# Reading the mLSTM normalisers ahead of all stages and loading each head's state matrix one background step before the sample chunk, in a one-core Trainium2 encoder layer

## The chip, the core and the metric

The kernel is one program on one core of one Trainium2 chip. The metric is the device time of one execution in microseconds (us), lower is better; the time of a kernel is the median of its runs. The engines of the core are named as the profile names them: PE (TensorE, matrix products; PEld is its weight load), DVE (VectorE), ACT (ScalarE), POOL (GpSimd) and SP (SyncE), whose queue issues every DMA of this kernel.

## The reference

One layer of a streaming encoder is computed for two streams: a prompt of 1024 tokens without history, and a sample of 64 tokens that continues a running stream. What matters here is the mLSTM branch: four heads of width 256, each with a matrix memory `C` (256 x 256), a normaliser `n` (256) and a running maximum `m`. A chunk of tokens reads the old memory and writes the new one:

```python
s = einsum(q, k) * w_intra
num = einsum(s, v) + w_inter[..., None] * einsum(q, C0)
den = sum(s, axis=-1) + w_inter * einsum(q, n0)
h = num / maximum(abs(den), exp(-m))[..., None]
C1 = decay * C0 + einsum(w_end, k, v)
n1 = decay * n0 + einsum(w_end, k)
```

For the prompt `C0`, `n0` start at zero. For the sample they are the inputs `state_C` and `state_n`. Both streams' final `C`, `n` and `m` are outputs.

## The kernel before

**Chunks.** The 1088 tokens of both streams (1024 and 64) stand side by side in the token dimension and are cut into three chunks of 384, 384 and 320. The input projection runs as units: one unit is one 128-column piece of `w_in`, and for each of the three chunks 24 matrix products (8 pieces of the contraction, three split products each, lines 326, 329 and 330) go into one PSUM tile `g` (three buffers). An operand is split into a high part (`...h`, by ACT) and a low part (`...l`, by DVE); `split`, lines 334 and 337, does both. So ACT writes `wh`, `Ch`, `smh` and DVE then writes `wl`, `Cl`, `sml`.

**Background steps.** After each chunk of a unit, `slot()` runs one step of the mLSTM generator of the current head, some steps of the depthwise convolution (each one DVE operation `acc` on 128x1118 elements) and one of a third generator. An mLSTM head takes nine chunks of 128 tokens (`c` = 0 to 7 the prompt, `c` = 8 the sample, 64 tokens) with two steps each. The first step of a chunk makes the products of q and k (`pS`), transposes k (`pk`) and prepares `sm`, `smh`, `sml`, `kwh`, `kwl`. The second transposes the last chunk's output (`out_gate`), then makes 15 products of width 258: three with `smh`/`sml` (`pN`), six with `Ch`/`Cl` (`pI`, the old memory), six with `kwh`/`kwl` (`pC`, the new memory), from which DVE writes the new `C`. So between two steps PE does the 24 products of a chunk.

**The state of the sample.** A tile `C` holds `C` in columns 0 to 255, `n` in column 256, and zeros behind. It has two buffers. After the second step of `c` = 7, lines 503 and 504 write the prompt's `C` and `n` out, the latter as 256 elements of 4 bytes. The first step of `c` = 8 takes the buffer that is free, loads `state_C` (256 KB, line 456) and `state_n` (256 elements of 4 bytes, line 457) into it and splits it (`csplit`).

**Order.** The program is written once and a scheduler orders each engine's instructions at build time; on the chip each engine goes through its own list strictly in order and waits at an instruction until what it needs is there. SP issues all DMAs in one list, and each takes the next of eight completion lanes in turn (`DMAHW0` to `DMAHW7` in the order's rows): an issue waits until the lane's earlier DMA has landed.

**Start.** `start_x` transposes x, loads the small vectors into rows of `vp` (`w_dw` first, then six rows), then the convolution cache `cp`. Behind these on SP stand a piece of `w_in` (`wr`, line 1109), the gate weights (into `fa`, line 219), the gate bias `bgb` and `state_m` (`smc`). `gates()` copies the gate weights into `wg` and multiplies (lines 238, 239).

Of the kernel before, what the change touches and what calls it, by code (L numbers as in the profile page):

```python
# [9 lines left out]
F32 = mybir.dt.float32  # L10
# [11 lines left out]
P = 128  # L22
KT = D // P
NH = 4
HD = 256
# [24 lines left out]
def hybrid_layer(ctx, tc, x_prompt, x_sample, cache_conv, state_C, state_n, state_m, w_in, b_gate,  # L50
# [3 lines left out]
    nc = tc.nc  # L54
    V, S, G, TE = nc.vector, nc.scalar, nc.gpsimd, nc.tensor
    w_in = w_in[0]

    def pool(name, bufs=1, stack=ctx, **kw):
        kw.setdefault("reuse_waits", "tile")
        if kw.get("space") is DRAM:  # L60
            kw.pop("reuse_waits")
        return stack.enter_context(tc.tile_pool(name=name, bufs=bufs, **kw))

    const = pool("const")
# [19 lines left out]
    def mtile():  # L84
        return pools["psm"].tile([P, 512], F32, tag="m", name="m")
# [37 lines left out]
            CREDIT["conv"] -= 1.0  # L123
        step("misc")

# [1 line left out]
    ident = const.tile([P, P], F32, name="ident")  # L127
    make_identity(nc, ident)
    vecs = const.tile([P, KT, NV], F32, name="vecs")
# [9 lines left out]
    dec = const.tile([P, NH, NT], F32, name="dec")  # L139
    bgb = const.tile([P, 8], F32, name="bgb")  # L140
    smc = const.tile([P, 1], F32, name="smc")

    proj = ExitStack()

# [1 line left out]
    XH, XL = [], []  # L146
    XO = {"h": XH, "l": XL}
    cv = pool("cv", stack=proj)
# [4 lines left out]
    def load_x(i):  # L153
        xt = xp.tile([P, D], F32, tag="x", name="x")
        nc.sync.dma_start(xt[:tile_len(i)], xrows(i))
        return xt

    def trans_x(i, xt):
        ci, off, n = i // 3, (i % 3) * P, tile_len(i)
        if i % 3 == 0:  # L160
            XH.append(ph.tile([P, KT, CN], F32R, tag="p", name="xh"))
            XL.append(pl.tile([P, KT, CN], F32R, tag="p", name="xl"))
        for kh in range(2):
            ps = mtile().rearrange("p (k t) -> p k t", k=4)
            for k in range(4):
                kk = kh * 4 + k
                TE.transpose(ps[:, k, :n], xt[:n, kk * P:(kk + 1) * P], ident[:n, :n])
            hi = XH[ci][:, kh * 4:kh * 4 + 4, off:off + n]
            S.activation(hi, ps[:, :, :n], AF.Copy)
            V.tensor_tensor(XL[ci][:, kh * 4:kh * 4 + 4, off:off + n], ps[:, :, :n], hi.bitcast(F32), ALU.subtract)  # L170
# [3 lines left out]
    def start_x():  # L174
        for i in range(3):
            trans_x(i, xt0[i])
            if i == 1:
                wsplit(0, True)
        for i in range(3, NT):
            trans_x(i, load_x(i))  # L180
        vp = xp.tile([NV, D], F32, tag="x", name="vp")
        nc.sync.dma_start(vp[0:CW, :], w_dw[0])
        for r, src in ((R_BDW, b_dw), (R_AG, ln_a_g), (R_AB, ln_a_b), (R_HN, hn_g), (R_G1, ln1_g), (R_B1, ln1_b)):
            nc.sync.dma_start(vp[r:r + 1, :], src[0:1, :])
        cp = xp.tile([CB, D], F32, tag="x", name="cp")
        nc.sync.dma_start(cp, cache_conv[0, 0])
        ps = mtile()
        for k in range(KT):
            TE.transpose(ps[:, k * NV:(k + 1) * NV], vp[:, k * P:(k + 1) * P], ident[:NV, :NV])
        V.tensor_copy(vecs, ps[:, :KT * NV].rearrange("p (k v) -> p k v", k=KT))  # L190
        ps = mtile()
        for k in range(KT):
            TE.transpose(ps[:, k * CB:(k + 1) * CB], cp[:, k * P:(k + 1) * P], ident[:CB, :CB])
        V.tensor_copy(cacheT, ps[:, :KT * CB].rearrange("p (k v) -> p k v", k=KT))

    N(start_x)

# [1 line left out]
    def gates():  # L199
        fa = fp.tile([P, 3072], F32, tag="f", name="fa")  # L200
        fb = fp.tile([P, 3072], F32, tag="f", name="fb")
# [102 lines left out]
            n = tile_len(b)  # L304
            V.tensor_copy(cols[:n, b:b + nb], ps[:n, 0:nb].rearrange("p c (h z) -> p c h z", z=32)[:, :, :, 0:4])

# [1 line left out]
    early, later = [], []  # L308

    def product(hi, lo, ci):  # L310
# [34 lines left out]
    def add_unit(w, c0, post):  # L345
        J(wcols(w, c0), lambda hi, lo: unit(hi, lo, post))

# [1 line left out]
    G32 = []  # L349
    HT = {}  # L350
    CVT = {}
# [67 lines left out]
    def mlstm(h):  # L419
        ml = pools["ml"]  # L420
        kf, qf, vh, vl, dt = HT["k"], HT["q"], HT["vh"], HT["vl"], HT["dt"]
        W = HD + 2
# [9 lines left out]

        def csplit(C):
            Ch = ml.tile([P, 2, W], F32R, tag="Ch", name="Ch")
            Cl = ml.tile([P, 2, W], F32R, tag="Cl", name="Cl")
            split(Ch, Cl, C)
            return Ch, Cl
# [7 lines left out]
                g = G32[ci][:, 2 * h + j, off:off + n]  # L445
                V.scalar_tensor_tensor(g, pT[:, j * P:j * P + n], vecs[:, 2 * h + j, R_HN:R_HN + 1], g, ALU.mult, ALU.mult)

        C = Ch = Cl = back = None
        nxt = prep(0)
        for c in range(NT):  # L450
            n, o = tile_len(c), c * P
            qs, ks = nxt
            if c == 8:
                C = ml.tile([P, 2, W], F32, tag="C", name="C", bufs=2)
                G.memset(C[:, :, HD + 1:], 0.0)
                nc.sync.dma_start(C[:, :, :HD], state_C[0, 0, h].rearrange("(j p) v -> p j v", p=P))
                nc.sync.dma_start(C[:, :, HD:HD + 1], state_n[0, 0, h].rearrange("(j p o) -> p j o", p=P, o=1))
                Ch, Cl = csplit(C)
            pS = mtile()
            for j in range(2):  # L460
                a = TE.matmul(pS[:, :2 * P], ks[:, j, 0, :], qs[:, j].rearrange("p e t -> p (e t)"), start=j == 0, stop=False)
# [38 lines left out]
            C = Cn  # L500
            if c >= 7:
                Cd, nd = (C_prompt, n_prompt) if c == 7 else (C_sample, n_sample)
                nc.sync.dma_start(Cd[0, 0, h].rearrange("(j p) v -> p j v", p=P), C[:, :, :HD])
                nc.sync.dma_start(nd[0, 0, h].rearrange("(j p o) -> p j o", p=P, o=1), C[:, :, HD:HD + 1])
            else:
                Ch, Cl = csplit(C)
            if c < 8:
# [13 lines left out]
            back = (c, n, isb)  # L521
# [97 lines left out]

    N(close_proj)  # L620

# [1 line left out]
    def set_operand(srcs, pad=False):  # L623
        H, L = [], []
        for ci, (_, n) in enumerate(CHUNKS):
# [18 lines left out]
        V.scalar_tensor_tensor(st[:n, 16:17], st[:n, 12:13], -1.0, st[:n, 15:16], ALU.mult, ALU.mult)  # L644
        return st[:n, 15:16], st[:n, 16:17]

# [1 line left out]
    A32, MB = [], []  # L648
    bra = ExitStack()

# [113 lines left out]
    for j in range(KT):  # L764
        add_unit(w_b_out[0], j * P, post_b(j))

# [1 line left out]
    wos = ExitStack()  # L768
    lns = ExitStack()
    WOH, WOL = [], []  # L770
# [23 lines left out]
    for j in range(KT):  # L794
        add_unit(w_a_out[0], j * P, post_ya(j))

# [1 line left out]
    X1H, X1L, Y2 = [], [], []  # L798
    last_ln = []

# [44 lines left out]

    N(out_proj)

# [1 line left out]
    stage[0] = 1  # L849
    NB = 4  # L850
    NBLK = 4 * KT // NB
# [156 lines left out]
        for jp in range(KT // 2):  # L1008
            wino_pair(blk, jp)

# [1 line left out]
    HID = {}  # L1012
    YT = []

# [82 lines left out]
        add_unit(w_ff1[0], u * P, post_h(u))  # L1097
    N(last_ff2)

# [1 line left out]
    pieces = [j for j in jobs if j[0] is not None]  # L1101
    raws, his = {}, {}
    now = [0]
# [7 lines left out]
    def wsplit(i, pinned=False):  # L1111
        if i < len(pieces) and i not in his and pieces[i][3] == now[0]:
            kind = pieces[i][2]
            w = KT * P if kind != "v" else 14 * P
            hi = pools["whl"].tile([P, w], F32R, tag="wh", name="wh")
            lo = pools["whl"].tile([P, w], F32R, tag="wl", name="wl")
            if kind != "v":
                split(hi, lo, raws[i], pinned=pinned)
                hi, lo = (t.rearrange("p (k n) -> p k n", n=P) for t in (hi, lo))
            else:  # L1120
                wino_weights(raws[i], hi, lo)
            his[i] = (hi, lo)
# [49 lines left out]
```

## Time and profile before

| | before |
|---|---|
| median of three runs | 2013.26 us (2011.92 to 2013.38) |
| the profiled execution's own span | 2012.8 us |
| PE busy | 1943.4 us, 97% |
| DVE busy | 1426.8 us, 71% |
| ACT busy | 648.7 us, 32% |
| POOL busy | 126.3 us, 6% |
| data moved by DMA | 131.06 MB, mean 65 GB/s |

The profile comes from one execution, 0.46 us shorter than the median, so durations from it can be set against the median as they are. A row of a time line has the start in us from the span's start, the duration, the engine, the line, the operation, out<-in with the tile names, and in square brackets the engine's idle time before it and what ended that. Matrix products are pipelined, so a product of 384 columns is shown with some 0.33 us while the next begins earlier. The granted clock of PE is 1.00 at 2.4 GHz and 0.50 at 1.2 GHz.

### The profile page before, as it was taken

The numbers are of one execution on the slowest core, as the hardware profiler recorded it, in microseconds if no ns is written. First come the engines' busy times: TensorE is split into PE (matmuls) and PEld (weight loads), VectorE is DVE, ScalarE is ACT, GpSimd is POOL, SyncE is SP. The second block draws the span as 40 slices with busy tenths as digits, with TensorE's granted clock in tenths as the row PEclk, the third lists the DMA queues.
The fourth block names the chain that finished last, engine by engine and source line by source line (L and its number), as shares of the span: only waits on it lengthen the run. The fifth ranks groups of instructions, "written<-read, shape, count | busy, mean of one in ns | idle before, by whom it ended". The sixth has DMA issues, their size and how long they took to land.

```text
span 2012.8 us, 30485 instructions
## 1 busy us (share of the span) xinstructions
PE 1943.4 (97%) x12395; PEld 1917.8 (95%) x12395; DVE 1426.8 (71%) x2717; ACT 648.7 (32%) x1209; POOL 126.3 (6%) x220
## 2 busy tenths in 40 slices
PE   8999899998999899989999998999999999999996
PEld 7999899998999899989999998999999999999995
DVE  4957776786678677868885557877686858677647
ACT  4323222333233323323342204524233332414232
POOL 1112210001000100000000000000000000000005
PEclk9999999999999999989999999999999999999998
DMA  4122321122112221225325310111111111111212
GB/s 148 44 78 67 85 70 43 54 67 47 56 41 63 62 63 37 64 66 172 116 82 154 116 40 21 32 53 43 53 42 54 43 43 53 43 53 43 74 42 79
DMA packets 174974, 131.06 MB, mean 65 GB/s; under 512 B 11518, under 2 KB 169694, under 8 KB 174833
## 3 DMA queue, kind: packets, MB, share of 16 engines
q1 hardware_dynamic: 174833, 129.11, 21.8%
q8 instruction: 97, 1.59, 0.3%
q14 instruction: 44, 0.36, 0.1%
HBM read 104.39 MB, written 24.63 MB: 64 GB/s over the span
## 4 chain that ended last, share of the span: by engine, by line
PE 80%; DVE 11%; DMA 4%; issue 2%; ACT 2%; POOL 1%; SPq 0%; POOLq 0%; ACTq 0%; DVEq 0%
PE g L326 25%; PE g L329 25%; PE g L330 25%; DMA C<-in_state_n_dram 2%; DVE s L668 2%; DVE acc L563 1%; PE m L326 1%; PE m L330 1%; PE m L329 1%; DVE o L1091 1%; DVE wl L337 1%; DVE ln L640 0%; DVE a L689 0%; DVE y L689 0%; DVE C L499 0%
## 5 line engine op out<-in xcount | busy, mean ns | idle before, releaser
L326 PE MATMUL g<-xh,wh 128*128 128x384 f32 (+1 forms) x1920 | 636.0, 331 | 0.0
L329 PE MATMUL g<-xl,wh 128*128 128x384 f32 (+1 forms) x1920 | 630.1, 328 | 0.0
L330 PE MATMUL g<-xh,wl 128*128 128x384 f32 (+1 forms) x1920 | 629.6, 328 | 0.0
L326 PEld LDWEIGHTS g<-xh,wh 128*128 128x128 f32 x1920 | 363.1, 189 | 0.4 <-ACT xh L334 0.2
L329 PEld LDWEIGHTS g<-xl,wh 128*128 128x128 f32 x1920 | 363.0, 189 | 0.3
L330 PEld LDWEIGHTS g<-xh,wl 128*128 128x128 f32 x1920 | 362.6, 189 | 0.1
L563 DVE SCALAR_TENSOR_TENSOR acc<-glu,vecs,acc 128x1118 f32<-128x1118 f32 x240 | 332.8, 1387 | 3.9
L334 ACT ACTIVATE wh<-wr 128x1024 fp32r<-128x1024 f32 (+1 forms) x168 | 166.1, 989 | 429.1 <-PE g L329 356.0
L337 DVE TENSOR_TENSOR wl<-wr,wh 128x1024 fp32r<-128x1024 f32 (+1 forms) x168 | 191.4, 1139 | 106.8 <-ACT wh L334 104.2
L326 PE MATMUL g<-x1h,wh 128*128 128x384 f32 (+1 forms) x768 | 253.1, 330 | 0.0
L329 PE MATMUL g<-x1l,wh 128*128 128x384 f32 (+1 forms) x768 | 252.8, 329 | 0.0
L330 PE MATMUL g<-x1h,wl 128*128 128x384 f32 (+1 forms) x768 | 252.6, 329 | 0.0
L329 PE MATMUL g<-hvl,wh 128*128 128x272 f32 x784 | 223.5, 288 | 0.0
L330 PE MATMUL g<-hvh,wl 128*128 128x272 f32 x784 | 221.5, 288 | 0.0
L326 PE MATMUL g<-hvh,wh 128*128 128x272 f32 x784 | 221.1, 289 | 0.1
L967 DVE TENSOR_TENSOR y<-g,y 128x272 f32<-128x272 f32 (+1 forms) x540 | 157.3, 341 | 26.8 <-PE g L330 25.1
L326 PEld LDWEIGHTS g<-hvh,wh 128*128 128x128 f32 x784 | 145.9, 189 | 1.7 <-DVE y L967 1.4
L329 PEld LDWEIGHTS g<-hvl,wh 128*128 128x128 f32 x784 | 147.4, 188 | 0.1
L330 PEld LDWEIGHTS g<-hvh,wl 128*128 128x128 f32 x784 | 146.4, 188 | 0.0
L330 PEld LDWEIGHTS g<-x1h,wl 128*128 128x128 f32 x768 | 144.8, 188 | 0.0
L329 PEld LDWEIGHTS g<-x1l,wh 128*128 128x128 f32 x768 | 144.7, 188 | 0.1
L326 PEld LDWEIGHTS g<-x1h,wh 128*128 128x128 f32 x768 | 144.5, 188 | 0.1
(267 smaller groups left out, 2440.9 us busy)
## 6 DMA issues: line engine op xcount, KB each, us to landing
wr<-in_w_in_dram SPq DMA_DIRECT2D x64, 512.0 KB
wr<-in_w_ff_dram SPq DMA_DIRECT2D x64, 512.0 KB
x<-in_x_prompt_dram SPq DMA_DIRECT2D x8, 512.0 KB
dwT<-acc SPq DMA_DIRECT2D x8, 512.0 KB
wr<-in_w_b_out_dram SPq DMA_DIRECT2D x8, 512.0 KB
wr<-in_w_a_out_dram SPq DMA_DIRECT2D x8, 512.0 KB
wr<-in_w_out_dram SPq DMA_DIRECT2D x8, 512.0 KB
out_dram<-o SPq DMA_DIRECT2D x16, 256.0 KB
```

What stands on the lines that cost most here:

```text
L326: first = TE.matmul(out, lh, rh, start=start, stop=False, skip_group_check=more)
L329: TE.matmul(out, lh, rl, start=False, stop=False, skip_group_check=more)
L330: TE.matmul(out, ll, rh, start=False, stop=stop, skip_group_check=more)
L334: a = S.activation(hi, src, AF.Copy)
L337: V.tensor_tensor(lo, src, hi.bitcast(F32), ALU.subtract)
L563: V.scalar_tensor_tensor(acc, glu[:, j:j + AC], vecs[:, c, j:j + 1], acc, ALU.mult, ALU.add))
L668: V.tensor_reduce(out[:, :n], t[:, :, :n].rearrange("p k t -> p t k"), AX.X, ALU.add)
L967: V.tensor_tensor(y, ps[:, pslc], y, ALU.add)
L1091: V.tensor_tensor(o[:n, hs], o[:n, hs], pools["g2"][:n, hs], ALU.mult)
```

## The change

`state_n` of all four heads goes into one small tile `snc`, by four loads in `start_x` between the rows of `vp` and `cp`. At the end of the second step of `c` = 7 the sample's tile is taken (`C0`), its matrix loaded, its last column zeroed and column 256 copied from `snc` on POOL. The sample chunk begins with an empty step (`yield`), and only then takes `C0` and splits it. The diff also removes comment lines, which stand as blank lines; these are left out below.

```diff
+    snc = const.tile([P, NH, 2], F32, name="snc")
...
             nc.sync.dma_start(vp[r:r + 1, :], src[0:1, :])
+        for h in range(NH):
+            nc.sync.dma_start(snc[:, h, :, None], state_n[0, 0, h].rearrange("(j p o) -> p j o", p=P, o=1))
         cp = xp.tile([CB, D], F32, tag="x", name="cp")
...
-        C = Ch = Cl = back = None
+        C = Ch = Cl = back = C0 = None
...
             if c == 8:
-                C = ml.tile([P, 2, W], F32, tag="C", name="C", bufs=2)
-                G.memset(C[:, :, HD + 1:], 0.0)
-                nc.sync.dma_start(C[:, :, :HD], state_C[0, 0, h].rearrange("(j p) v -> p j v", p=P))
-                nc.sync.dma_start(C[:, :, HD:HD + 1], state_n[0, 0, h].rearrange("(j p o) -> p j o", p=P, o=1))
+                yield
+                C = C0
                 Ch, Cl = csplit(C)
...
                 nc.sync.dma_start(nd[0, 0, h].rearrange("(j p o) -> p j o", p=P, o=1), C[:, :, HD:HD + 1])
+                if c == 7:
+                    C0 = ml.tile([P, 2, W], F32, tag="C", name="C", bufs=2)
+                    nc.sync.dma_start(C0[:, :, :HD], state_C[0, 0, h].rearrange("(j p) v -> p j v", p=P))
+                    G.memset(C0[:, :, HD + 1:], 0.0)
+                    G.tensor_copy(C0[:, :, HD:HD + 1], snc[:, h, :, None])
```

**PE, ahead of head 0's sample products.** Before, the last chunk in front of them ends so; each chunk of 24 products is shown by its last three rows, `m<-ident,isb` is `out_gate` of `c` = 7, `m<-vh,smh` the first of the 15 products:

```order
L326 MATMUL g<-xh,wh 128x320
L329 MATMUL g<-xl,wh 128x320
L330 MATMUL g<-xh,wl 128x320
L443 MATMUL m<-ident,isb 128x128 x2
L326 MATMUL m<-vh,smh 128x258
L329 MATMUL m<-vl,smh 128x258
L330 MATMUL m<-vh,sml 128x258
```

The same place after the change (lines are three or more higher):

```order
L329 MATMUL g<-xh,wh 128x320
L332 MATMUL g<-xl,wh 128x320
L333 MATMUL g<-xh,wl 128x320
L462 MATMUL m<-qs,ks 128x256
L465 MATMUL m<-qs,ks 128x128
L462 MATMUL m<-qs,ks 128x256
L465 MATMUL m<-qs,ks 128x128
L468 MATMUL m<-ident,k 128x128 x2
L329 MATMUL g<-xh,wh 128x384
L332 MATMUL g<-xl,wh 128x384
```

The products of q and k, which stood before the 320 chunk, now stand behind it, and a whole chunk of 384 stands between them and the sample's 15 products, in all four heads.

**ACT, around `Ch` of head 0's sample.** `s` is the eviction of a projection chunk, `wh` the split of the next weight piece, `sm` the first operation on the products of q and k. Before:

```order
L575 ACTIVATE s<-g 128x384
L471 ACTIVATE sm<-m 128x128
L339 ACTIVATE kwh<-m,cols 128x256
L334 ACTIVATE Ch<-C 128x516
L334 ACTIVATE smh<-sm 128x128
L334 ACTIVATE wh<-wr 128x1024
L575 ACTIVATE s<-g 128x320
```

After:

```order
L581 ACTIVATE s<-g 128x384
L337 ACTIVATE Ch<-C 128x516
L337 ACTIVATE wh<-wr 128x1024
L581 ACTIVATE s<-g 128x320
L472 ACTIVATE sm<-m 128x128
L342 ACTIVATE kwh<-m,cols 128x256
L337 ACTIVATE smh<-sm 128x128
```

`Ch`, which needs the loaded state, stood behind `sm` and `kwh`; it now stands ahead of both, with `wh` and an eviction between.

**DVE, the same place.** Before:

```order
L563 SCALAR_TENSOR_TENSOR acc<-glu,vecs,acc 128x1118
L472 TENSOR_TENSOR sm<-m,sm 128x128
L473 TENSOR_TENSOR sm<-sm,dt 128x128
L340 SCALAR_TENSOR_TENSOR kwl<-m,cols,kwh 128x256
L337 TENSOR_TENSOR Cl<-C,Ch 128x516
L337 TENSOR_TENSOR sml<-sm,smh 128x128
```

After:

```order
L340 TENSOR_TENSOR Cl<-C,Ch 128x516
L340 TENSOR_TENSOR wl<-wr,wh 128x1024
L473 TENSOR_TENSOR sm<-m,sm 128x128
L343 SCALAR_TENSOR_TENSOR kwl<-m,cols,kwh 128x256
L474 TENSOR_TENSOR sm<-sm,dt 128x128
L569 SCALAR_TENSOR_TENSOR acc<-glu,vecs,acc 128x1118
L340 TENSOR_TENSOR sml<-sm,smh 128x128
```

Here too `sm`, `kwl` and `sml` stood around `Cl`; they now stand behind it, `wl` and, for `sml`, `acc`.

**SP at the start, with what each issue waits for.** `DMAHW3_49` is the lane that the load of `w_dw` took. Before:

```order
L186 DMA cp<-in_cache_conv_dram 30x1024 [waits DMAHW2_49,PE_49]
L1109 DMA wr<-in_w_in_dram 128x8x128 [waits DMAHW3_49,DVE_49]
L219 DMA fa<-in_w_in_dram 128x8x8 [waits DMAHW4_49]
L220 DMA bgb<-in_b_gate_dram 128x8 [waits DMAHW5_49]
L223 DMA smc<-in_state_m_dram 1x1 [waits DMAHW6_49]
```

After:

```order
L187 DMA snc<-in_state_n_dram 128x2x1 [waits DMAHW2_49]
L187 DMA snc<-in_state_n_dram 128x2x1 [waits DMAHW3_49]
L187 DMA snc<-in_state_n_dram 128x2x1 [waits DMAHW4_49]
L187 DMA snc<-in_state_n_dram 128x2x1 [waits DMAHW5_49]
L189 DMA cp<-in_cache_conv_dram 30x1024 [waits DMAHW6_49,PE_49]
L1115 DMA wr<-in_w_in_dram 128x8x128 [waits DMAHW7_49,DVE_49]
L222 DMA fa<-in_w_in_dram 128x8x8 [waits DMAHW0_49]
```

The wait for the lane of `w_dw` stood at `wr`; it now stands at the second of the four new loads, and `cp`, `wr` and `fa` are behind it. In the heads SP's list is the same as before but for the load of `state_n`, which is gone: the load of the matrix still stands right behind the two outputs of the prompt's state.

## Rows read from the trace of the kernel before

**Rows 1.** The page, share of the chain that ended last by line.

```profile
PE g L326 25%; PE g L329 25%; PE g L330 25%; DMA C<-in_state_n_dram 2%; DVE s L668 2%; DVE acc L563 1%; PE m L326 1%; PE m L330 1%; PE m L329 1%; DVE o L1091 1%; DVE wl L337 1%; DVE ln L640 0%; DVE a L689 0%; DVE y L689 0%; DVE C L499 0%
```

**Rows 2.** Time line of PE: the four heads' sample products, then two short waits.

```profile
246.05 0.58 PE L326 MATMUL m<-vh,smh 128*128 128x258 f32 x1 [6.50 <-ACT smh L334]
246.78 0.58 PE L330 MATMUL m<-vh,sml 128*128 128x258 f32 x1
...
461.52 0.58 PE L326 MATMUL m<-vh,smh 128*128 128x258 f32 x1 [5.85 <-ACT smh L334]
...
674.06 0.58 PE L326 MATMUL m<-vh,smh 128*128 128x258 f32 x1 [6.51 <-ACT smh L334]
...
886.89 0.58 PE L326 MATMUL m<-vh,smh 128*128 128x258 f32 x1 [7.28 <-ACT smh L334]
...
1008.89 0.37 PE L704 MATMUL m<-mean,sl 128*128 128x2 f32 x1 [2.17 <-DVE sl L337]
...
1204.40 0.27 PE L704 MATMUL m<-mean,sl 128*128 128x2 f32 x1 [2.28 <-DVE sl L337]
```

**Rows 3.** Windows, PE alone: stretch; us, PE busy (products), granted clock, DMA share, GB/s.

```profile
246.05:251.00 4.95, 4.95 (x20) 0.51 0.11 38
461.52:466.10 4.58, 4.58 (x19) 0.51 0.12 39
674.06:677.54 3.48, 3.48 (x14) 0.50 0.13 47
886.89:892.75 5.86, 5.86 (x22) 0.51 0.21 57
1010.44:1014.00 3.56, 3.56 (x13) 0.50 0.69 207
1205.24:1208.00 2.76, 2.76 (x17) 1.00 0.20 59
```

**Rows 4.** Windows, line 326 alone: a 384 chunk of head 0, with weight loads.

```profile
230.84:235.00 4.16, 2.69 (x8) 1.40 (x8) 1.00 0.94 262
```

**Rows 5.** Time line of ACT, head 0.

```profile
245.16 0.63 ACT L334 ACTIVATE Ch<-C 128x516 fp32r<-128x516 f32 x1 [8.84 <-DMA C<-in_state_n_dram]
...
245.90 1.04 ACT L334 ACTIVATE wh<-wr 128x1024 fp32r<-128x1024 f32 x1
246.85 0.41 ACT L575 ACTIVATE s<-g 128x320 f32<-128x320 f32 x1
```

**Rows 6.** Time line of DVE, head 0.

```profile
237.62 0.29 DVE L473 TENSOR_TENSOR sm<-sm,dt 128x128 f32<-128x128 f32 x1
237.83 0.48 DVE L340 SCALAR_TENSOR_TENSOR kwl<-m,cols,kwh 128x256 fp32r<-128x256 f32 x1
...
246.65 1.38 DVE L563 SCALAR_TENSOR_TENSOR acc<-glu,vecs,acc 128x1118 f32<-128x1118 f32 x1
...
248.46 1.22 DVE L337 TENSOR_TENSOR wl<-wr,wh 128x1024 fp32r<-128x1024 f32 x1
```

**Rows 7.** Time line of SP, head 0: the normaliser's output, the state matrix's load.

```profile
232.88 0.46 SPq L504 DMA_DIRECT2D out_dram<-C  x1
233.39 0.49 SPq L456 DMA_DIRECT2D C<-in_state_C_dram  x1
```

**Rows 8.** Windows without an engine, head 0: us, granted clock, DMA share, GB/s.

```profile
236.00:243.30 7.30, 1.00 0.15 15
```

**Rows 9.** DMA packets of the stretch 243.30 to 245.16, head 0.

```profile
DMA packets 419, 0.20 MB, mean 107 GB/s; under 512 B 269, under 2 KB 419, under 8 KB 419
```

**Rows 10.** Time line of SP at the start.

```profile
19.60 0.32 SPq L186 DMA_DIRECT2D cp<-in_cache_conv_dram  x1
25.44 0.40 SPq L1109 DMA_DIRECT2D wr<-in_w_in_dram  x1
25.89 0.58 SPq L219 DMA_DIRECT2D fa<-in_w_in_dram  x1
```

**Rows 11.** Time line of PE at the start: the first product of the gates.

```profile
30.74 0.44 PE L238 MATMUL g<-xh,wg 128*128 128x384 f32 x1 [1.66 <-DVE wg L232]
```

## The prediction

> **What bounds the kernel now.** I read the chain that ended last first. By line it is the projection products three times over, and behind them one transfer: the load of `state_n` with 2% of the span, some 40 us [rows 1]. PE is the bound, so time can only be won where PE stands idle or runs slowly. PE's time line shows such a place once in each head, ahead of the sample's 15 products: 6.50, 5.85, 6.51 and 7.28 us of idle time, together 26.1 us [rows 2]. ACT shows why: it waited 8.84 us at `Ch` for that load, `smh` stands behind `Ch` on ACT, and PE began 0.89 us after `Ch` (246.05 − 245.16) [rows 2, 5].
>
> A second loss hides behind the idle time. Right after each of the four waits PE runs at a granted clock of 0.50 or 0.51, which is 1.2 GHz, for 4.95, 4.58, 3.48 and 5.86 us [rows 3]. At full clock these stretches would have taken half, so the slow clock costs 0.49 × 15.39 + 0.50 × 3.48 = 9.3 us. Shorter waits are not all alike: behind one of 2.17 us the clock is 0.50, behind one of 2.28 us it is 1.00 [rows 2, 3]. At stake in the heads are thus 26.1 + 9.3 = 35.4 us, 1.8% of the span.
>
> **The heads: one more chunk in front.** The order puts a full 384 chunk between the products of q and k and the sample's 15 products, in all four heads. Such a chunk takes 4.16 us at full clock [rows 4]. PE gets that work while the load runs, so the wait shrinks by 4.16 us per head. The work is not new; it is taken from behind the sample products.
>
> **The heads: how much sooner the state is there.** The matrix's load is issued at the same place of SP's list as before, right behind the output of `n_prompt`: 232.88 the output, 233.39 the load [rows 7]. So "loaded ahead" here means that others wait longer for it; its issue is not earlier. What is gone is the load of `state_n` behind it. Its 256 elements of 4 bytes are nearly all of the 269 packets under 512 B that moved from 243.30 to 245.16, the last 1.86 us before `Ch` began [rows 5, 9]. The long part lies before: from 236.00 to 243.30 the engines were busy to 0.15 and moved 15 GB/s [rows 8], so no want of bandwidth held the matrix; what crawls there must be the 256 single elements of the output of `n_prompt`, and they are still in front. I bound the gain by 0 (the matrix itself was last) and 1.9 us (the whole stretch of elements goes) and take the middle, 0.9 us per head.
>
> The Trainium skill, page "DMA: Bandwidth & Descriptors", section "Queues, rings and completion order", says that a DMA's semaphore increment lands only after every earlier write of that DMA engine; by that rule the matrix can't be reported before the output in front of it, and the 10 us between issue and report remain, as the crawl in [rows 8] suggests.
>
> **The heads: what the new order costs.** Before, `sm`, `kwh` and `kwl` were done while ACT waited, and only `smh` (PE at `Ch` + 0.89) and `sml` were left; the third product, the first that needs `sml`, stood at 246.78, `Ch` + 1.62 [rows 2, 5]. Now `Ch` is ahead of them in ACT's list. After the state's arrival there follow `Ch` 0.63, `wh` 1.04, on DVE `wl` 1.22 (which stands ahead of the first `sm`), `kwl` 0.48, two small operations of 0.29, `smh` of about the same length: 4.2 us, of which some 0.1 overlaps [rows 5, 6]. The eviction of the 320 chunk, 0.41, runs on ACT beside `wl`. So the first product stands at about `Ch` + 4.1. `sml` also has an `acc` of 1.38 us in front, which puts the third product at about `Ch` + 5.25. That is 5.25 − 1.62 = 3.63 us later than before, and PE waits for it: all 24 products of the extra chunk are done by then. PE has nothing else in its list, since it goes in order.
>
> Per head: 4.16 + 0.9 − 3.63 = 1.43 us gained (0.5 to 2.4 by the bounds on the arrival); four heads 5.7 us (2.1 to 9.7). The wait that is left is some 4 us before the first product and another 0.7 at the third, longer than the 2.17 us behind which the clock was 0.50, so I leave the slow stretches as they are.
>
> **The start.** The four new loads stand ahead of `cp`, `wr` and `fa` on SP. Before, `cp` was issued at 19.60 and `wr` had to wait until 25.44, for the lane of `w_dw` [rows 10]. Now the second new load has that wait. From 25.44 three issues of about 0.5 us (232.88 to 233.39) [rows 7] and one of `cp` (0.45, as `wr` to `fa`) come first: `wr` at about 27.4, `fa` at about 27.85, 1.96 us later than 25.89 [rows 10]. The gates' first product waited for these weights at 30.74, with 1.66 us of idle time in front [rows 11], so 2.0 us go straight on PE. The transposes of `cp` wait too, but inside the same time. The wait of some 3.7 us then reaches into the lengths behind which the clock fell; that costs between 0 and 2.9 us (half of the longest slow stretch, 5.86) [rows 3], and I take 2.0, near their mean of 9.3/4. Start: −4.0 us (2.0 to 4.9), and up to 4 more if the new loads are slow to move, see below.
>
> **What costs nothing.** The zeroing and the copy of column 256 are small POOL operations, and the copy needs only `snc`, which is there 200 us before; POOL is idle for nearly the whole span and the matrix takes 10 us to come. They lie under that transfer; without this cover they would add their own length to `Ch`. The convolution steps behind `out_gate` come later by a step or two and lie under projection chunks.
>
> **Sum.** 5.7 − 4.0 = 1.7 us faster. The profiled execution is 2012.8 us, 0.5 us less than the median, too little to correct for: 2013.26 − 1.7 = 2011.6 us. A measurement of this kernel can tell about 0.2%, 4 us, from no change, so this is "same".
>
> **Rivals.** *The matrix comes fast.* If the element load of `state_n` was what held the transfers, then without it the matrix lands soon after its issue, some 6 us before PE wants it. All idle time and all slow stretches of the heads go: −35.4 + 4.0 = −31.4, 1981.9 us. For it speaks that ACT waited for just that load [rows 5]; against it that the element packets moved at the very end [rows 9], so the 7.3 us of crawl before are not theirs. The Trainium skill's "Rules for kernel authors" on the same page (issue early, compute, wait late) promises this too; no row here shows the matrix early.
>
> *The clock stays up in the heads.* If the arrival gains the full 1.9 us and DVE's list has slack that I don't see (`acc` done while it waits), the waits fall to 2 to 3 us, and some of them keep 2.4 GHz, as the one of 2.28 us did [rows 2, 3]. That gives 9.7 us and up to 9.3 more, on average 13: 2013.26 − 13 + 4 = 2004 us.
>
> *Slower, by the start.* Element loads stretch: the 256 elements of one `state_n` took up to 1.86 us [rows 9]. Three of them lie ahead of `wr` and `fa` in the DMA engines; if each holds what is behind it for that long, 3 × (1.86 − 0.5) = 4.1 us come on top. With the slow clock behind: 2.0 + 4.1 + 2.9 = 9.0 us lost, against 4 from the heads: 2018.3 us. It decides if the gates' first product stands later than about 34.5 us instead of 30.74, with the heads at their lower half.
>
> *The load ahead is none.* This is my forecast: the matrix stays behind the elements of `n_prompt`, and the gain is the moved chunk less the new order.
>
> **How the numbers follow.** Chances: forecast 0.56, with 2007 to 2016 for itself; the clock stays up 0.17; slower by the start 0.18; the matrix comes fast 0.09. The range runs from 2001 (past the second rival) to 2019 (past the third) and leaves out the fast matrix, 0.09, and some 0.07 at the upper end. Faster by over 0.2% means below 2009.2: the fast matrix 0.09, the clock 0.15, a lower edge of the forecast 0.06, together 0.30. Slower means above 2017.3: 0.16 of the third rival and 0.02 else, together 0.18. Same: 0.52.
>
> **What would show it.** In the changed kernel's trace: `Ch` waits for `state_C`'s load and starts about 10.5 to 11.5 us after its issue, as now 11.8 (245.16 − 233.39) [rows 5, 7]; PE's idle time ahead of the sample products is 4 to 4.5 us, with a further 0.5 to 1 at the third; granted clock 0.5 behind it; the first product of the gates at 32.5 to 33.5 us. `Ch` within 4 us of the issue would prove the first rival, granted clock 1.00 behind the sample products the second, gates beyond 34.5 us the third. My sum fails most easily at DVE's order: if the scheduler's list gives way less than 3.6 us per head, because `wl` waits or `acc` is long done, every 1 us counts four times.

## The result, and the profile after

| | before | after |
|---|---|---|
| median | 2013.32 us (2011.92 to 2017.00) | 2023.49 us (2022.89 to 2025.08) |
| span of the profiled execution | 2012.8 us | 2021.8 us |
| ratio after / before | | 1.0050 (1.0036 to 1.0065) |

The changed kernel is 10.2 us slower, outside the range; the spans of the two profiled executions differ by 9.0 us. One run of `a1_pad32` below took 2708.79 us at a mean granted clock of 0.65 and is left out of its median. The page of the changed kernel shows PE busy for longer, with the same number of instructions as before (12395, and 1943.4 us):

```profile
PE 1954.5 (97%) x12395; PEld 1927.8 (95%) x12395; DVE 1428.6 (71%) x2717; ACT 642.3 (32%) x1205; POOL 123.4 (6%) x224
```

So the loss is not one of waiting. PE's waits ahead of the sample products did become shorter. Time line of PE after, the four heads' first and third sample products (compare [rows 2]):

```profile
253.80 0.58 PE L329 MATMUL m<-vh,smh 128*128 128x258 f32 x1 [3.70 <-ACT smh L337]
255.99 0.58 PE L333 MATMUL m<-vh,sml 128*128 128x258 f32 x1 [1.39 <-DVE sml L340]
...
468.29 0.44 PE L329 MATMUL m<-vh,smh 128*128 128x258 f32 x1 [4.42 <-ACT smh L337]
470.48 0.58 PE L333 MATMUL m<-vh,sml 128*128 128x258 f32 x1 [1.54 <-DVE sml L340]
...
684.82 0.58 PE L329 MATMUL m<-vh,smh 128*128 128x258 f32 x1 [5.41 <-ACT smh L337]
687.01 0.58 PE L333 MATMUL m<-vh,sml 128*128 128x258 f32 x1 [1.39 <-DVE sml L340]
...
900.69 0.58 PE L329 MATMUL m<-vh,smh 128*128 128x258 f32 x1 [5.19 <-ACT smh L337]
...
901.85 0.58 PE L333 MATMUL m<-vh,sml 128*128 128x258 f32 x1 [0.36 <-DVE sml L340]
```

Together these are 23.4 us, where the four waits of before were 26.1.

Where the time goes is found by following one event through both traces. ACT splits the weight pieces (`wh`) in the same order in both kernels, one per unit. How much later the same split starts after than before:

| split number | before, us | after, us | later by, us | what lies in between |
|---|---|---|---|---|
| 3 | 43.82 | 48.61 | 4.79 | the start |
| 15 | 205.61 | 211.88 | 6.27 | 12 units |
| 19 | 277.94 | 279.84 | 1.90 | 4 units, head 0's sample |
| 31 | 440.19 | 443.97 | 3.78 | 12 units |
| 35 | 501.61 | 507.32 | 5.71 | 4 units, head 1's sample |
| 45 | 635.51 | 642.87 | 7.36 | 10 units |
| 49 | 701.89 | 711.50 | 9.61 | 4 units, head 2's sample |
| 61 | 864.14 | 875.61 | 11.47 | 12 units |
| 63 | 903.89 | 913.35 | 9.46 | 2 units, head 3's sample |
| 71 | 1002.50 | 1013.02 | 10.52 | 8 units |
| 85 | 1293.94 | 1302.90 | 8.96 | branch A's norm, 8 units, output projection |
| 195 | 1903.61 | 1912.59 | 8.98 | feed-forward |

Between the heads, where nothing was changed, each unit falls behind by 0.16 us: 1.88 us in the 12 units from split 19 to 31, 1.86 from 49 to 61. In the feed-forward stage nothing changes any more. So the projection's products themselves take longer. A unit holds 48 products of 384 columns; here is one such pair of chunks without any wait in it, in the kernel before and then in the changed one. The row has the stretch, its length in us, PE's busy time (records that reach into the stretch are counted too), the granted clock, the DMA share and GB/s:

```profile
82.02:90.34 8.32, 8.32 (x51) 1.00 0.02 3
```

```profile
86.98:95.47 8.49, 8.49 (x51) 1.00 0.03 6
```

8.32 against 8.49 us for 48 products, both at a granted clock of 1.00. As a mean over the time line from 100 to 1000 us the products follow each other every 0.1734 us before and every 0.1767 after; the 320-column products have 0.147 us in both. Over 80 units that is 80 x 48 x 3.3 ns = 12.7 us.

What in the change can do that? The only thing that touches every unit is the tile `snc`. It has 32 bytes per partition, stands in the constants' pool, and moves every tile behind it by 32 bytes. In the built programs `xh` starts at byte 5664 before and 5696 after, `xl` at 42528 and 42560, while the weights `wh` and `wl`, which are allocated from the other end, stay at 212960 and 221152. That was the theory for the experiments. The rival: the added work itself (order, loads, waits) slows the products.

### The profile page after: what moved, and what is told of

The parts are those of the page before. It is cut to its first block, busy times and chain, and to the rows that moved or that the text cites. A ratio compares the mean times of both kernels' runs of the same rounds, so it can differ in the third digit from the quotient of the medians.

```text
span 2021.8 us, 30493 instructions
## 1 busy us (share of the span) xinstructions
PE 1954.5 (97%) x12395; PEld 1927.8 (95%) x12395; DVE 1428.6 (71%) x2717; ACT 642.3 (32%) x1205; POOL 123.4 (6%) x224
## 4 chain that ended last, share of the span: by engine, by line
PE 45%; DVE 7%; ACT 1%; issue 1%; POOL 1%; DMA 1%; POOLq 0%; ACTq 0%; DVEq 0%
PE g L329 15%; PE g L332 15%; PE g L333 15%; DVE s L674 2%; DVE o L1097 1%; DMA C<-in_state_C_dram 1%; DVE ln L646 0%; DVE a L695 0%; DVE y L695 0%; PE m L1057 0%; ACT o L1096 0%; POOL ln L713 0%; POOL ln L649 0%; DVE mb L759 0%; DVE wl L340 0%
```

## The experiments

Changes are named by the kernel that they start from. Times are medians, compared with the kernel before on the same chip.

**Placement alone.**

```diff
     smc = const.tile([P, 1], F32, name="smc")
+    padc = const.tile([P, 8], F32, name="padc")
```

> The kernel before with one unused tile of 32 bytes behind smc in the constants' pool, and nothing else: no instruction added, and every SBUF tile allocated behind it on the left side (the operands xh and xl among them) 32 bytes further, as snc does it in the changed kernel. Address theory: the projection's products of 384 columns follow each other at 0.1766 us instead of 0.1734 (as in the changed kernel's trace), 3840 products x 3.2 ns = 12.3 us, so 2024 to 2026 us, less a few us that later waits on DVE take back: 2021 to 2026. Rival theory (the slower products come from the changed kernel's own work: its instructions, loads or order): 0.1734 and 2013.3 us, unchanged.

Measured 2024.36 against 2012.08 us, ratio 1.0063 (1.0043 to 1.0083). An unused tile of 32 bytes costs 12.3 us. The same pair of chunks in this kernel:

```profile
81.93:90.41 8.48, 8.48 (x51) 1.00 0.03 7
```

**The change without the placement.** `snc` moves to the right side of SBUF, where it displaces nothing:

```diff
-    snc = const.tile([P, NH, 2], F32, name="snc")
+    snc = pool("snp", stack=proj, side="right").tile([P, NH, 2], F32, name="snc")
```

> The changed kernel with the same tile snc allocated on the other side of SBUF, ahead of the projection's weight tiles, so that xh, xl and all other operands lie where they lay before the change. Address theory: products at 0.1734 us, and what is left is the start (+4.8 us measured in the changed kernel) and the heads (about -4.4): 2011 to 2015 us. Rival theory: 0.1766 and about 2023.5 us as the changed kernel.

Measured 2015.80 against 2012.08 us, ratio 1.0015 (1.0006 to 1.0025). The pair of chunks is back at 8.32 us:

```profile
86.44:94.76 8.32, 8.32 (x50) 1.00 0.02 6
```

The added work does not slow the products; the place of the operands does. What is left of the change is a loss of 3.7 us (interval 1.2 to 5.0).

**Is it the operand's place, or its distance to the weights?**

> The kernel before with 32 unused bytes on the right side, ahead of the projection's weight tiles wh and wl, which so lie 32 bytes lower, while xh and xl stay. If the moving operand's own address decides (xh, xl): 0.1734 and 2013.3 us. If it is where operand and weights stand to each other: another spacing, slower by up to 12 us: 2013 to 2026.

Ahead of the pool `whl`, which holds `wh` and `wl`:

```diff
+    pool("rpad", side="right").tile([P, 8], F32, name="padr")
```

> The kernel before with an unused tile of 64 bytes instead of 32 behind smc: xh and xl start at 32 modulo 64 again, as before, but at 96 instead of 32 modulo 128. If the address modulo 64 decides: 0.1734 and 2013.3 us. If modulo 128 or the distance to the weights decides: another spacing, 0.1766 or between, 2013 to 2026 us.

`a4_pad64` has `padc` with 16 columns instead of 8. Moving the weights alone, by 32 bytes, is as bad as moving the operand: 2025.85 against 2012.08 us, ratio 1.0067 (1.0052 to 1.0082). With 64 bytes in front of the operand: 2021.75 us, 1.0048 (1.0031 to 1.0065). So the operand's own place does not decide alone, nor does its place modulo 64. The pairs of chunks, `a3_weights32` and then `a4_pad64`:

```profile
84.29:92.77 8.48, 8.48 (x51) 1.00 0.03 7
```

```profile
82.54:91.00 8.46, 8.46 (x51) 1.00 0.04 7
```

Taken as distance of `xh` from `wh` modulo 256, before has 64, after, `a1` and `a3` have 96, `a4` has 128. The feed-forward stage of the kernel before also has 128, and its 48 products also take longer, 8.45 us. Three tests follow from that: the changed kernel with its weights moved so that distance 64 comes back (`c2`, and `d1`, which was written when `c2` had missed), and the feed-forward's weights, with what is allocated behind them, moved to distance 64 (`c3`).

> The changed kernel untouched, but for 96 unused bytes on the right side, ahead of the weight tiles: operands xh, xl stay where the change put them (64 modulo 128), the weights wh, wl move from 96 to 0 modulo 128, so that the distance between the two is again 64 modulo 128, as in the kernel before. If the distance decides: products of 384 columns at 0.1734 us and about 2015.8 us, as a2_snc_right. If the operand's own place decides: 0.1766 and 2023.5 us.

> The kernel before with 64 unused bytes ahead of the weight tiles of the feed-forward stage, where operand and weights both stand at 32 modulo 128 and the products of 384 columns follow each other at 0.176 us. With the weights at 96, the distance is 64 modulo 128 as in the projection. If that distance is the fast one everywhere: 0.1734 there, 1536 products x 2.6 ns = 4.0 us, 2008 us. If not: 0.176 and 2012 us.

> The changed kernel untouched, but for 224 unused bytes on the right side ahead of the weight tiles. Then xh, xl stand at 64 and wh, wl at 0 modulo 256, a distance of 64 as in the kernel before (32 and 224), while both lie elsewhere. If the distance modulo 256 decides: products of 384 columns at 0.1734 us and about 2014 to 2016 us, as a2_snc_right. If absolute places decide: another spacing, and 2017 to 2025 us.

`c2` is the changed kernel with `padr` of 24 columns, `d1` with 56. `c3`, on the kernel before, is:

```diff
+        pool("lpad").tile([P, 16], F32, name="padl")
         pools["whl2"] = pool("whl2", 2)
```

`c2` expected distance 64 modulo 128; modulo 256 it has 192, which I had overlooked. It came out between: 2018.86 against 2011.82 us, ratio 1.0033 (1.0022 to 1.0045). Pairs of chunks take one of two lengths here; two neighbouring units, and two later ones:

```profile
84.31:92.79 8.48, 8.48 (x50) 1.00 0.03 6
96.31:104.64 8.33, 8.33 (x51) 1.00 0.24 63
276.34:284.82 8.48, 8.48 (x50) 1.00 0.23 62
288.34:296.66 8.32, 8.32 (x50) 1.00 0.25 63
```

Units take the two weight buffers in turn, and both stand at 128 modulo 256. The buffer does not decide: in the built program the first and the last of these four units use one buffer, the two in the middle the other. So at this distance something counts besides the value modulo 256, and no run shows what.

`d1` has 64 modulo 256 with the operand where the change put it: 2015.59 against 2011.17 us, ratio 1.0019 (1.0009 to 1.0030), as `a2`, and the products are fast:

```profile
85.35:93.67 8.32, 8.32 (x50) 1.00 0.01 3
```

`c3` makes the feed-forward's products as fast as the projection's: 2009.42 against 2011.82 us, ratio 0.9981 (0.9970 to 0.9992). A pair of its 384 chunks, in the kernel before and then in `c3`:

```profile
1347.83:1356.28 8.45, 8.45 (x50) 1.00 0.23 65
```

```profile
1342.58:1350.90 8.32, 8.32 (x50) 1.00 0.23 66
```

> The kernel before with 192 unused bytes behind smc: xh, xl and wh, wl both stand at 224 modulo 256, distance 0. The distances seen so far gave 0.1734 us (64), 0.1766 (96), 0.1760 (128) and 0.1748 (192). If the distance decides, 0 gives a fifth value, which no run foretells; at 0.173 to 0.177 us 2012 to 2026 us.

`d3` (`padc` with 48 columns) gave 2013.22 against 2011.17 us, ratio 1.0009 (0.9999 to 1.0020). All placements of the projection, with the mean spacing from 100 to 1000 us:

| kernel | xh mod 256 | wh mod 256 | distance | spacing, us | ratio |
|---|---|---|---|---|---|
| before | 32 | 224 | 64 | 0.1734 | 1 |
| d1_after_dist64 | 64 | 0 | 64 | 0.1733 | 1.0019 |
| a2_snc_right | 32 | 224 | 64 | 0.1734 | 1.0015 |
| d3_dist0 | 224 | 224 | 0 | 0.1740 | 1.0009 |
| c2_after_shifted | 64 | 128 | 192 | 0.1748 | 1.0033 |
| a4_pad64 | 96 | 224 | 128 | 0.1760 | 1.0048 |
| a1_pad32 | 64 | 224 | 96 | 0.1767 | 1.0063 |
| a3_weights32 | 32 | 192 | 96 | 0.1767 | 1.0067 |
| after | 64 | 224 | 96 | 0.1767 | 1.0050, 1.0056 |

The two distances that were placed in two ways, 64 and 96, gave the same spacing both times, and 128 gave nearly the same in `a4_pad64` (8.46 us) as in the feed-forward stage of before (8.45). Why, the runs do not show. PE's weight loads run beside its products (in the page above PEld is busy for 1927.8 us, PE for 1954.5), and that both read SBUF at once is a possible meeting point, but this is argued.

**Do the parts add?**

> The changed kernel itself, beside the others on one chip, to set its parts against it: the operand's place (a1_pad32 measured +12.6 us alone) and the rest (a2_snc_right, +3.7 us alone). If they add, about 2028 us against 2012; measured first was 2023.5 against 2013.3, so that some 5 us would be taken back at later waits.

The changed kernel beside the others: 2022.93 against 2011.17 us, ratio 1.0056 (1.0036 to 1.0077), 11.8 us. `a1` (12.3, interval 8.7 to 16.7) and `d1` (4.4, interval 1.8 to 6.0) make 17. In the table of splits above the changed kernel takes 1.6 us back from split 71 to 85. That is no property of the place: the trace of `a1` has the same slow products and falls 1.2 us further behind there. The mean granted clock of this stretch is 0.99 in the changed kernel, 0.97 in `a1` and before. With these intervals the difference of 5 us is not settled further.

**The other parts.** `b1_heads_only` is `a2` with `state_n` loaded at each head's start; `b2_start_only` the kernel before with the four early loads and nothing else. `b1`, on `a2`, where the four loads leave `start_x`, in `head_start`:

```diff
         drain("mlstm")
+        nc.sync.dma_start(snc[:, h, :, None], state_n[0, 0, h].rearrange("(j p o) -> p j o", p=P, o=1))
```

> The change without its start: snc on the right side (nothing else is shifted), each head's state_n loaded where that head begins, 150 us and more ahead of its use, so that nothing new stands on SP ahead of cp, the weights and the gate weights. The heads as in the changed kernel. By the sum from the traces (start +4.4 us at equal operand addresses): a2_snc_right less 4.4, that is about the time of the kernel before, 2009 to 2013 us; the gates' first product again at about 30.7 us at full clock. If the start were not what costs, it would stay near a2_snc_right, 2015.8 us.

> The start alone: the kernel before with the four loads into snc (on the right side) ahead of cp, and snc not used; the heads load their state as before. Start theory: +4.4 us, about 2016.5 us, the gates' first product at about 33 us with the granted clock at 0.50 behind it for about 6 us. If the early loads are harmless: 2012.1 us.

`b1`: 2011.51 against 2012.10 us, ratio 0.9993 (0.9983 to 1.0002). The heads' part of the change gains 0.6 us, nothing that can be told from zero. `b2`: 2013.84 us, ratio 1.0011 (1.0001 to 1.0021), a loss of 1.7 us (interval 0.2 to 4.2); between `b1` and `a2`, which differ by the start alone but were measured on two chips, lie 4.3 us. In both kernels with early loads, the gates' first product stands at 32.8 us, in `b1` at 30.0, as expected. So the start costs 2 to 4 us.

**The late element load alone.** In the kernel before, column 256 is copied from `snc` (on the right side, loaded at each head's start) instead of loaded behind the matrix:

```diff
-                nc.sync.dma_start(C[:, :, HD:HD + 1], state_n[0, 0, h].rearrange("(j p o) -> p j o", p=P, o=1))
+                G.tensor_copy(C[:, :, HD:HD + 1], snc[:, h, :, None])
```

> The kernel before, but column 256 copied from snc (loaded at the head's beginning, right side) instead of loaded behind the matrix: the removal of state_n's late load alone, without the step ahead. If the late element load cost what I took, 0.9 us per head (0 to 1.9): 2012.1 less 3.6, and no new order on ACT and DVE: 2004 to 2012 us, Ch at 10 to 11 us behind the issue of the matrix.

2011.66 against 2012.10 us, ratio 0.9994 (0.9985 to 1.0004). The wait from the matrix's issue to `Ch` shrank from 11.9 to 10.9 us as a mean of the heads (10.12, 10.87, 11.93, 10.48); I had taken 0.9 us. In the trace PE's waits ahead of the sample products fell from 26.1 to 22.8 us, and 0.7 us came back at head 0's `out_gate`. The median shows no such gain, but its interval (3.0 us faster to 0.8 slower) doesn't exclude it.

**The matrix ahead of the single elements.** In `b1`, the load of the matrix and the output of `n_prompt` change places:

```diff
                 nc.sync.dma_start(Cd[0, 0, h].rearrange("(j p) v -> p j v", p=P), C[:, :, :HD])
-                nc.sync.dma_start(nd[0, 0, h].rearrange("(j p o) -> p j o", p=P, o=1), C[:, :, HD:HD + 1])
...
+                nc.sync.dma_start(nd[0, 0, h].rearrange("(j p o) -> p j o", p=P, o=1), C[:, :, HD:HD + 1])
```

> b1_heads_only with two issues of SP exchanged: the load of the state matrix stands ahead of the output of n_prompt instead of behind it. Theory of the elements in front (the 256 single elements of n_prompt's output hold the matrix up): Ch starts some 3 to 5 us after the issue instead of 10, long before PE wants it; the four waits of PE (23 us in the changed kernel) and the slow clock behind them go: 2012 less 25 to 36, 1976 to 1988 us. Rival (256 KB behind the 256 KB output of C_prompt and the weight load take that long anyway): no change against b1_heads_only, about 2011 us.

2002.46 against 2012.10 us, ratio 0.9951 (0.9931 to 0.9970): 9.6 us faster, less than half of what the theory said. The transfer behaved as it said. The matrix's issue on SP and `Ch` on ACT, head 0:

```profile
234.68 0.47 SPq L506 DMA_DIRECT2D C<-in_state_C_dram  x1
```

```profile
237.70 0.64 ACT L335 ACTIVATE Ch<-C 128x516 fp32r<-128x516 f32 x1 [0.20 <-DMA C<-in_state_C_dram]
```

3.0 us instead of 10 to 12, one swap of two issues; in heads 1 and 2 `Ch` did not wait at all and began 3.1 us after the issue. In head 3 it still waited, and began 7.8 us after the issue (870.09); no run shows why:

```profile
877.90 0.64 ACT L335 ACTIVATE Ch<-C 128x516 fp32r<-128x516 f32 x1 [4.62 <-DMA C<-in_state_C_dram]
```

The first three heads agree with the Trainium skill, page "DMA: Bandwidth & Descriptors", section "Queues, rings and completion order", by which a load's report waits for the earlier writes on its DMA engines; the swap takes those writes from in front of it.

But PE's idle time moved. It now stands ahead of the sample's `out_gate`, in three of the four heads:

```profile
263.72 0.47 PE L445 MATMUL m<-ident,isb 64*128 64x64 f32 x2 [5.92 <-DVE isb L524]
...
474.72 0.47 PE L445 MATMUL m<-ident,isb 64*128 64x64 f32 x2 [4.58 <-DVE isb L524]
...
687.26 0.47 PE L445 MATMUL m<-ident,isb 64*128 64x64 f32 x2 [7.34 <-DVE isb L524]
```

These are 17.8 us, and behind them PE runs slowly again:

```profile
263.72:269.00 5.28, 5.28 (x17) 0.50 0.45 121
```

DVE's `isb` needs the inverse square root of the sample's norm, which POOL makes (`st`). POOL's time line shows what is ahead of that:

```profile
250.14 1.37 POOL L386 PARTITION_BROADCAST dt<-negM  x1 [8.73 <-DVE st L520]
260.56 0.85 POOL L363 TENSOR_TENSOR xs<-xh,xl 128x320 f32<-128x320 f32 x1 [9.05 <-issue]
261.39 0.25 POOL L521 TENSOR_SCALAR st<-st 64x1 f32<-64x1 f32 x1
261.63 0.85 POOL L363 TENSOR_TENSOR xs<-xh,xl 128x320 f32<-128x320 f32 x1
262.44 0.59 POOL L522 TENSOR_TENSOR st<-st,mhalf 64x1 f32<-64x1 f32 x1
```

The next head's broadcast runs first, and then POOL does nothing for 9.05 us, waiting for nothing that the profile shows. This order is not new. The kernel before has it too, and 8.05 us of the same idle time:

```profile
248.41 2.49 POOL L384 PARTITION_BROADCAST dt<-negM  x1 [12.18 <-issue]
258.95 0.25 POOL L516 TENSOR_SCALAR st<-st 64x1 f32<-64x1 f32 x1 [8.05 <-issue]
...
260.03 0.59 POOL L517 TENSOR_TENSOR st<-st,mhalf 64x1 f32<-64x1 f32 x1
```

Counted from the matrix's issue, the root ends after 27.2, 26.1 and 26.4 us in heads 0 to 2 of the kernel before, and after 28.4, 26.5 and 29.2 us in `b3`. PE was ready for `out_gate` after 27.7, 27.2 and 27.4 us before, held up by the load and the slow clock, and waited in head 0 alone, for 1.81 us. In `b3` it is ready after 23.1, 23.5 and 23.5 us, so POOL is what it waits for now.

**The square root ahead of the broadcast.** On `b3`, an edge for the scheduler that orders the two on POOL:

```diff
-            G.tensor_tensor(st[:n, 12:13], st[:n, 3:4], mhalf[:n], ALU.pow)
+            HT["root"] = G.tensor_tensor(st[:n, 12:13], st[:n, 3:4], mhalf[:n], ALU.pow)
...
-        G.partition_broadcast(dt.rearrange("p c t -> p (c t)")[:, :T], negM[32 * h:32 * h + 1, :])
+        cast = G.partition_broadcast(dt.rearrange("p c t -> p (c t)")[:, :T], negM[32 * h:32 * h + 1, :])
+        if "root" in HT:
+            tc.add_manual_dep(cast.ins, HT["root"].ins.name, mybir.DependencyInfo(
+                mybir.DependencyClass.NoSync, mybir.DependencyReason.DATA), reason="order")
```

> b3_matrix_first with one order more: on POOL the inverse square root of the sample's norm stands ahead of the next head's broadcast of the decay row, behind which POOL stood some 9 us before its next work in b3's trace. There PE waited for it 5.92, 4.58 and 7.34 us at the sample's out_gate in heads 0 to 2. Theory (this wait ate what the early matrix gave): those waits and the slow clock behind them go, 17.8 us and some 6 more, less what the later broadcast costs at the next head: 2002.5 less 12 to 22, 1980 to 1990 us. Rival: the broadcast, now later, holds the next head's first chunk instead: 2000 us as b3.

1976.18 against 2011.82 us, ratio 0.9825 (0.9808 to 0.9841): 35.6 us faster than the kernel before, and 26 us below `b3`, where 12 to 22 were expected. POOL now makes the root first, and its idle time of 8.81 us, now ahead of the broadcast, holds nobody on the path:

```profile
250.24 0.56 POOL L525 TENSOR_TENSOR st<-st,mhalf 64x1 f32<-64x1 f32 x1
259.61 1.36 POOL L386 PARTITION_BROADCAST dt<-negM  x1 [8.81 <-issue]
```

PE's waits for `smh` fall to 1.0 us over the whole program (the row gives the total in us, the times, the longest), and in that view no row for `out_gate` is left:

```profile
PE m L327 <- ACT smh L335: 1.0, 2, 0.6
```

The edge changed PE's list as well: in heads 0 to 2 the built program has 24 projection products between the sample's products and its `out_gate`, where `b3` and the kernel before have 64. So `c1` tests the two orders together. Not tested is what the swap of the issues and this edge give in the kernel before, without the rest of the change.

> c1_root_first and c3_ff_weights64 together, as a version against both kernels: 1976 to 1986 us if both theories hold; the gain of c1 alone if only that one does.

`c4` puts `c1` and `c3` together: 1974.64 against 2011.82 us, ratio 0.9810 (0.9795 to 0.9824). It is the fastest kernel of this study; its distance to `c1` is inside the intervals.

## Why the prediction was wrong, point by point

**What failed: a term that was not in the sum.** "The start" and "What costs nothing" price the loads into `snc` and the copy from it; the sum has nothing for the tile itself. Its 32 bytes lengthened the 384-column products of the projection by 3.3 ns on average, 12.7 us in all, of which 6 to 8 us remain in the time (after less `a2` or `d1`). None of the rivals held it, and no row shown ahead of the prediction held it: it is a property of where tiles lie, which the built program tells. One sign was in the trace of before: 48 products of one size take 8.32 us in the projection and 8.45 in the feed-forward. With distance 64 restored, the same change measures 2015.6 to 2015.8 us, inside the range I gave and 3.7 to 4.4 us above the kernel before.

**What bounds the kernel, and the stake: right.** 35.4 us at the four waits and the slow clock behind them was what I set; `c1`, which removes both, gains 35.6 (interval 32 to 39). That the two agree to 0.2 us is luck: my sum left out the wait of 1.81 us at head 0's `out_gate` and a slow stretch of 3.4 us behind it (264.60 to 268.00, granted clock 0.50).

**The chunk in front: right.** It takes 8.49 / 2 = 4.24 us after, against 4.16.

**The arrival: right within its bounds.** From the matrix's issue to `Ch` before 11.8, 11.5, 12.2 and 12.3 us, after 10.1, 11.4, 12.3 and 11.4: 0.6 us gained as a mean, where 0.9 was taken. The reason given, the elements of `n_prompt` in front, is shown by `b3`.

**The new order: too cheap.** The first product came at `Ch` + 4.02 (253.80 − 249.78), as worked out (4.1). The third came at + 6.21 in heads 0 to 2 (255.99 − 249.78), where I had 5.25, and at + 5.19 in head 3. The difference is one operation. `Ch` on ACT, `sml` on DVE and POOL's broadcast after, head 0:

```profile
249.78 0.63 ACT L337 ACTIVATE Ch<-C 128x516 fp32r<-128x516 f32 x1 [7.77 <-DMA C<-in_state_C_dram]
```

```profile
253.33 1.38 DVE L569 SCALAR_TENSOR_TENSOR acc<-glu,vecs,acc 128x1118 f32<-128x1118 f32 x1
254.62 1.32 DVE L340 TENSOR_TENSOR sml<-sm,smh 128x128 fp32r<-128x128 f32 x1
```

```profile
253.98 1.95 POOL L387 PARTITION_BROADCAST dt<-negM  x1 [8.06 <-DVE sm L474]
```

`sml` took 1.32 us instead of some 0.29, and ended within 0.01 us of the broadcast (255.94 and 255.93); so in heads 1 and 2. Head 3 has no next head, no broadcast, and no such delay. The Trainium skill, page "SBUF — State Buffer", section "Summary: rules for kernel authors", has a rule that fits: of a DVE operation with two SBUF inputs and a GpSimd operation that reads SBUF, the second to issue waits until the first ends. The three heads agree with it; no run took the broadcast away alone, but in `b3`, where it lies elsewhere, `sml` takes 0.28 to 0.29 us. Per head the term is 6.21 − 1.62 = 4.59 us instead of 3.63, and the gain 4.24 + 0.6 − 4.59 = 0.3 us instead of 1.4; in head 3 it is 4.24 + 0.6 − 3.57 = 1.3. Two new waits of PE at the sample's `out_gate`, 0.70 and 0.97 us in heads 1 and 2, stand against the one of 1.81 us in head 0 before. That makes some 2 us of gain in the heads instead of 5.7; `b1` measured 0.6, with an interval from 0.4 us slower to 3.4 us faster. This second error is smaller than the first.

**The slow clock: right.** The waits that were left kept it. Windows of PE alone after, the gates and the four heads' sample products:

```profile
33.03:38.80 5.77, 5.77 (x19) 0.53 0.26 77
253.80:260.86 7.06, 5.67 (x23) 0.54 0.29 83
468.29:475.84 7.55, 6.01 (x24) 0.55 0.34 97
684.82:690.82 6.00, 4.61 (x19) 0.54 0.31 88
900.69:905.80 5.11, 4.75 (x20) 0.54 0.48 141
```

At about 0.46 of the busy time of the last four (21.0 us) this costs 9.7 us, as before (9.3 in the four stretches of [rows 3]).

**The start: right.** The four loads took SP from 20.64 to 27.16, and the gates began 2.3 us later than in [rows 11], inside the 32.5 to 33.5 us that I gave:

```profile
20.64 6.52 SPq L187 DMA_DIRECT2D snc<-in_state_n_dram  x4
27.26 0.42 SPq L189 DMA_DIRECT2D cp<-in_cache_conv_dram  x1
...
28.20 0.57 SPq L222 DMA_DIRECT2D fa<-in_w_in_dram  x1
```

```profile
33.03 0.69 PE L241 MATMUL g<-xh,wg 128*128 128x384 f32 x1 [2.52 <-DVE wg L235]
```

Of the 4.8 us in the trace, 2 to 4 us remain in the timed kernels (`b2`, and `a2` less `b1`); I took 4.0. So the third rival was not it: the gates never came near 34.5 us.

**The rivals.** The fast matrix was real, but for another reason than the change: the swap in `b3` makes it, not the removal of `state_n`, which `b4` puts at 1.1 us. And its full price is paid only with the second step, `c1`.

## What to carry to other kernels

A new tile, even an unread one of 32 bytes, moves every tile behind it. Before a change with a new tile is costed, compare the addresses of the operands of the costliest products in both built programs, and put small tiles where they displace nothing. When a load is late though little data moves, look at what was issued just in front of it: here 256 single elements, and a swap of two issues (`b1` to `b3`, 9 us) was worth more than the whole change. And when a wait is taken away, name the next one on the same path before the gain is counted: `b3` got 9.6 of 35.6 us until POOL's order was changed too.

## What the runs showed of the hardware

- Products of 128x384 f32 on PE follow each other every 0.1733 to 0.1767 us on average at a granted clock of 1.00, by the distance between the streamed operand and the weights in SBUF modulo 256: fastest at 64, slowest of those tried at 96. Products of 320 columns stayed at 0.147 us in the projection. At distance 192 some pairs of chunks took 8.48 us and others 8.32 or 8.33, on either weight buffer, so the distance modulo 256 is not all.
- An output of 256 elements of 4 bytes holds up a 256 KB load issued behind it: 10 to 12 us from the issue to its reader with the output in front, 3.0 to 3.1 us with it behind in three heads, 7.8 us in the fourth.
- Between a broadcast on POOL and the next TENSOR_SCALAR or TENSOR_TENSOR there POOL idles for 7 to 9 us, which ends by nothing that the profile shows (8.05 us before, 7.36 after, 9.05 in `b3`); in `c1`, 8.81 us of such idle time stand ahead of the broadcast.
